# One more 512-column projection through seven half-size products, and eight small products of linear attention put in another order

## The chip, the cores and the metric

The kernel runs on one core of a Trainium2 chip (trn2). The metric is device microseconds of one execution of the whole program, the median of several runs. Inputs, weights and output lie in the chip's memory; the core works from its on-chip memory (SBUF), with matmul results in PSUM. Five engines run side by side, each through its own queue in order: TensorE (PE, with its weight loads shown apart as PEld), VectorE (DVE), ScalarE (ACT), GpSimd (POOL) and SyncE (SP), which only issues transfers.

## The reference

One layer on 512 tokens of width 1024, all in float32. What matters here:

```
h = rmsnorm(x)
hq, hk, hv, hr, ha, hatt, hgate = split(h @ w_in)
# A: gated linear attention, chunks of 64 tokens, 4 heads (dk 128, dv 256)
attn = where(causal, q_dec @ k_in.T, 0);  o = attn @ v + q_dec @ state
# B: dilated attention, 3 head groups with dilation 1, 4, 16, 4 heads each
logits = q @ k.T * hd**-0.5 + bias; softmax; @ v; groups merged by their denominators
x = x + (sigmoid(gA) * (oA @ w_o_gla) + sigmoid(gB) * (oB @ w_o_attn)) @ w_out
x = x + relu(rmsnorm(x) @ w_mlp1)**2 @ w_mlp2
x = x + sigmoid(rmsnorm(x) @ w_pg) * (p @ w_pp);  out = rmsnorm(x)
```

"The second group's keys" (k1) are the 512 columns of `h @ w_in` that give the keys of the group with dilation 4.

## The kernel before, in words

Every large product is made in three passes: both operands are split into a high and a low part (`hi` on ACT by a copy to float32r, `lo` on DVE by a subtraction), and hi·hi, hi·lo and lo·hi are added up in PSUM.

A projection of 512 columns is done in one of two ways. `fm` makes one 128-column tile at a time: 8 pieces of the contraction x 3 passes = 24 matmuls of 128x128 weights with 512 moving columns, so 96 for four tiles. `strassen` makes the whole projection as a 2x2 block product by seven half-size products (`STAGES`: A11·B11, S1·T1, A22·T4, S2·T2, A12·B21, S4·B22, S3·T3): each stage is 24 matmuls of 128x128 weights with 256 moving columns, 168 in all. S1 to S4 are sums of weight blocks, T1 to T4 sums of blocks of the normalised input. The T's are made once, by the generator `xsums`, and used by all such projections. Results of the stages stand in four PSUM banks; ACT copies one out after stages 1 to 4 (`begin`), DVE adds the second half (`finish`, in `heads` by `add`).

Weights come as 512 KB units through a ring of `NRAW` = 6 buffers, in the order of `OPERANDS`. `fetch(i+2)`, called as operand i's matmuls begin, issues `lo` of operand i+2, `hi` of i+3, weight sums of i+4 (`sums`) and the load of i+5 (`prepare`). For a projection with seven products, `EARLY` puts the load of block A21 and, on POOL, an adding transfer of A22 into the same buffer (S1) five operands ahead. `sums` makes S2 and S4 on DVE in place, and S3 by an adding transfer on POOL.

Smaller work runs as generators in the list `side`: after each piece of 8 matmuls `run` calls `step`, which takes one step of one generator (two take turns) and pops one item from `later`. `drain()` issues all that is left. So each engine's order is fixed by this program order.

The order around the change: q0 (group 0's queries, begun while the input is read), k0, then `scores0` (group 0's scores: 8 pieces of PE work, each followed by a softmax on DVE and ACT) and `xsums` go on `side`; q1 and k1 run by `fm` under them (`qk_cls`, lines 989 and 990); a drain; q2 and k2 by `heads`/`strassen`; then `scores12`, which reads q1, k1, q2, k2. At the start, POOL's power operation (line 375) gives the scale of the first normalisation; its broadcast goes through the two matmuls of lines 410 and 411.

In `gla` (once for each of the four heads) the chunk scores take eight float32 matmuls of 64 moving columns into `pa`: four with 128 weight columns (line 889) and four with 64 (line 891), in turn. A float32 matmul shows as two records in the trace.

Of the kernel before, what the change touches and what calls it, by code (L numbers as in the profile page):

```python
# [14 lines left out]
OP = mybir.AluOpType  # L15
# [19 lines left out]
def att_col(g, which):  # L35
    return ATT + (g * 3 + which) * 512
# [5 lines left out]
def weight_units():  # L42

    u = []

    def fm(name, src, col, n, row=0):
        for j in range(n):
            u.append((f"{name}.{j}", "fm", src, row, col + j * P))

    def tm(name, src, col):  # L50
        for i in range(4):
            u.append((f"{name}.{i}", "tm", src, i * 2 * P, col))

    fm("q0", "w_in", att_col(0, 0), 4)
    u = u[NS:]
    def quad(name, src, col, kind="quad"):
        for m, k in ((0, 0), (1, 0), (1, 1), (0, 1)):
            u.append((f"{name}.A{m + 1}{k + 1}", kind, src, k, col + m * (P if kind == "quad" else 256)))

    fm("k0", "w_in", att_col(0, 1), 4)  # L60
    fm("q1", "w_in", att_col(1, 0), 4)
    fm("k1", "w_in", att_col(1, 1), 4)
    quad("q2", "w_in", att_col(2, 0))
    quad("k2", "w_in", att_col(2, 1))
    quad("v1", "w_in", att_col(1, 2), "quadt")
    quad("v2", "w_in", att_col(2, 2), "quadt")
    quad("v0", "w_in", att_col(0, 2), "quadt")
    quad("gq", "w_in", GQ)
    quad("gk", "w_in", GK)
    quad("gv0", "w_in", GV, "quadt")  # L70
    for j in range(4):
        u.append((f"oa.{j}", "half", "w_o_attn", 0, j * 2 * P))
    quad("r0", "w_in", GR)
    quad("gv1", "w_in", GV + 512, "quadt")
    quad("r1", "w_in", GR + 512)
    for i in range(2):
        quad(f"gb{i}", "w_in", GATE + D + i * 512)
    for i in range(2):
        quad(f"ga{i}", "w_in", GATE + i * 512)
    fm("og", "w_o_gla", 0, 8)  # L80
    fm("wo", "w_out", 0, 8)
    for q in range(8):
        quad(f"m1q{q}", "w_mlp1", q * 512)
    for sub in range(2):
        for kk in range(16):
            u.append((f"m2s{sub}.{kk}", "tm", "w_mlp2", kk * 2 * P, sub * 512))
    for j in range(2):
        u.append((f"pp{j}.0", "tm", "w_pp", 0, j * 512))
    for j in range(2):
        tm(f"pg{j}", "w_pg", j * 512)  # L90
    return u
# [50 lines left out]
def block_kernel(ctx, tc, xT, ws, pT, wts, wha, wa2, vec, lnf, rel, onehot, ident_d, mask_d, out):  # L142
    nc = tc.nc
    V, S, TE, SY, GP = nc.vector, nc.scalar, nc.tensor, nc.sync, nc.gpsimd
# [11 lines left out]
    def u32(name="u"):  # L156
        return ar.tile([P, T], F32, tag="u", name=name)

    def u32r(name="ur"):
        return ar.tile([P, T], F32R, tag="u", name=name)  # L160
# [8 lines left out]
    side, later = [], []  # L169
# [13 lines left out]
    def drain():  # L183
        while side or later:
            step()
# [20 lines left out]
    def sums(i):  # L206
        q, _, what = OPERANDS[i].rpartition(".")
        if what == "S2":
            w = raw[f"{q}.S2"] = raw[f"{q}.S1"]
            V.tensor_tensor(w, w, raw[f"{q}.A11"], op=OP.add)  # L210

            w = raw[f"{q}.S3"] = raw[f"{q}.A11"]
            GP.dma_start(w, wts[UNIT[f"{q}.A21"]], accum_op=OP.add)  # L213
        elif what == "S4":
            w = raw[f"{q}.S4"] = raw[f"{q}.S2"]
            V.tensor_tensor(w, w, raw[f"{q}.A12"], op=OP.add)  # L216
# [73 lines left out]
    def halves(t):  # L290
        return slice(t * HT, (t + 1) * HT)
# [52 lines left out]
    def split_hi(x, col=None):  # L344
        hi = u32r()
        if col is None:
            S.activation(hi, x, AF.Copy)  # L347
        else:
            S.activation(hi, x, AF.Copy, scale=col)
        return hi  # L350

    def split_lo(x, hi, col=None):
        lo = u32r()
        if col is None:
            V.tensor_tensor(lo, x, hi.bitcast(F32), op=OP.subtract)  # L355
        else:
            V.scalar_tensor_tensor(out=lo, in0=x, scalar=col, in1=hi.bitcast(F32), op0=OP.mult, op1=OP.subtract)
        return hi, lo
# [64 lines left out]
    for k in range(KC):  # L423
        t = u32()
        SY.dma_start(t[:, 0:NS * P + 1], ws[k])
        wr.append(t)
        t = u32()
# [23 lines left out]
    for k in range(KC):  # L451
        x, ln = xr[k], wr[k][:, NS * P:NS * P + 1]
        hi, lo = u32r(), u32r()
# [27 lines left out]
    xn, xs, tx = [], [None] * KC, {}  # L481
# [12 lines left out]
    def minus(o, a, b):  # L494

        V.scalar_tensor_tensor(out=o, in0=a, scalar=-1.0, in1=b, op0=OP.mult, op1=OP.subtract)

    def xsums():
        for g in range(2):
            t1, t2, t3, t4 = (u32() for _ in range(4))  # L500
            for p in range(2):
                x0, x1 = (xn[4 * g + 2 * p + k][0] for k in range(2))
                o = halves(p)
                V.tensor_tensor(t1[:, o], x0[:, halves(0)], x0[:, halves(1)], op=OP.subtract)
                minus(t2[:, o], t1[:, o], x1[:, halves(1)])
                yield
                V.tensor_tensor(t3[:, o], x1[:, halves(1)], x0[:, halves(1)], op=OP.subtract)
                minus(t4[:, o], t2[:, o], x1[:, halves(0)])
                yield
            names, ts, hi = ("T1", "T2", "T3", "T4"), (t1, t2, t3, t4), [split_hi(t1)]  # L510
            for i in range(4):
                if i < 3:
                    hi.append(split_hi(ts[i + 1]))
                tx[names[i], g] = split_lo(ts[i], hi[i])
                yield

    def xs_op(name, pr):
        if name in ("B11", "B21", "B22"):
# [74 lines left out]
    def qk_cls(name, scale):  # L593

        res = []
        for j in range(4):
            o, ps = u32(), fm(f"{name}.{j}", xs)
            S.activation(c3(o), cm(ps), AF.Copy, scale=scale)
            res.append(o)
        return res  # L600

    def heads(name, scale, cls=False):

        res = [u32() for _ in range(4)]

        def finish(m, t, s, ps):
            for n in range(2):
                o, a, b = res[2 * n + m], s[:, halves(n)], ps[:, halves(n)]
                if cls:
                    o, a, b = c3(o)[:, :, t * 64:(t + 1) * 64], cm(a), cm(b)  # L610
                else:
                    o = o[:, halves(t)]
                add(m, o, a, b, scale)

        strassen(name, xs_op, finish, scale=scale)
        return res
# [85 lines left out]
    def scores0():  # L702
        for h in range(4):
            for bp in range(2):
                ps = smt()
                for a in range(2):
                    b = 2 * bp + a
                    lo = 0 if b else P
                    TE.matmul(ps[:, a * 256 + lo:a * 256 + 256], lhsT=q0[h][:, b * P:(b + 1) * P],  # L709
                              rhs=k0[h][:, (b - 1) * P + lo:(b + 1) * P], start=True, stop=True)  # L710
                yield
                pr = u32()
                softmax(ps, P if bp == 0 else 0, bias0[h], st0[:, 0, :], st0[:, 1, :], h * 4 + bp * 2, pr)
                p0.append(pr)
# [130 lines left out]
    def gla(h):  # L845
        b, q, k = gb_[h], gq[h], gk[h]
# [5 lines left out]
                        op=OP.subtract)  # L852
        V.tensor_tensor(ea8[:, 1::2, :], b8[:, 1::2, 63:64].to_broadcast([P, 4, 64]), b8[:, 1::2, :],
                        op=OP.subtract)
# [33 lines left out]
        for p in range(4):  # L888
            TE.matmul(pa[:, p * P + 64:(p + 1) * P], lhsT=kx[:, p * P:(p + 1) * P],  # L889
                      rhs=q[:, p * P + 64:(p + 1) * P], start=True, stop=True)  # L890
            TE.matmul(pa[0:64, p * P:p * P + 64], lhsT=k[:, p * P:p * P + 64],  # L891
                      rhs=q[:, p * P:p * P + 64], start=True, stop=True)
        qh = split_hi(qp)
# [90 lines left out]
    q0 = [qk0_evac(p, HD_SCALE) for p in q0ps + [q0t]]  # L984
    k0 = [qk0_evac(fm(f"k0.{j}", xsr), 1.0) for j in range(4)]
    drain()
    side.append(scores0())
    side.append(xsums())
    q1 = qk_cls("q1", HD_SCALE)
    k1 = qk_cls("k1", 1.0)  # L990
    drain()
    q2 = heads("q2", HD_SCALE, True)
    k2 = heads("k2", 1.0, True)
    drain()
# [91 lines left out]
    for j in range(KC):  # L1086
        t = u32()
# [83 lines left out]
    def quad(q):  # L1171


        def finish(m, t, s, ps):
            add(m, s, s, ps)

            def positive():
                V.tensor_scalar(s, s, 0.0, None, op0=OP.max)  # L1178

            def act():  # L1180
                for n in range(2):
                    j = 4 * q + 2 * n + m
                    if hid[j] is None:
                        hid[j] = u32()
                    S.activation(hid[j][:, halves(t)], s[:, halves(n)], AF.Square)  # L1185

            later.extend([positive, act])

        def extra(i):
            if i in (3, 4):  # L1190
                later.append(lambda: hid_split(i - 3))

        strassen(f"m1q{q}", x1_op, finish, extra=extra if q == 7 else None)
# [14 lines left out]
    for sub in range(2):  # L1208
        pss = [mmt() if sub == 0 else smt() for _ in range(4)]
        for kk in range(16):  # L1210
# [11 lines left out]
            if sub == 1 and kk == 8:  # L1222
                for k in range(2):
                    t = u32()
                    GP.dma_start(t, pT[k * P:(k + 1) * P, :])
                    pt.append(split(t))
                for g in range(2):
                    t = u32()
                    GP.dma_start(t, lnf[:, g * 512:(g + 1) * 512].to_broadcast([P, 512]))
                    lnb.append(t)  # L1230
        for o in range(4):
            j = 4 * sub + o
            t = u32()
# [189 lines left out]
```

## Time and profile before

| | |
|---|---|
| median of 3 runs | 979.17 us (978.92 to 979.62) |
| profiled execution, its own time | 979.68 us |
| its span in the trace | 977.9 us |
| mean granted TensorE clock | 0.998 |
| PE busy / PEld busy | 968.3 us (99%) / 885.3 us (91%) |
| DVE / ACT / POOL busy | 685.9 us (70%) / 522.6 us (53%) / 94.6 us (10%) |
| memory traffic | 133.63 MB, mean 137 GB/s |

The span runs from the first to the last instruction in the trace; the execution's own time has 1.78 us more around it. A line "L250 PE MATMUL mmt<-ur,hi" is a matmul issued by line 250 into tile mmt from tiles ur and hi. In the timeline the columns are start, duration, engine and line, and "x2" means two records merged. A matmul's recorded duration overlaps its neighbours', so the pace of PE is read from starts.

### The profile page before, as it was taken

What the parts mean: (1) busy time and instruction counts of PE and PEld (TensorE: products, weight loads), DVE (VectorE), ACT (ScalarE), POOL (GpSimd) and SP (SyncE); (2) the same over time, 40 slices, a digit from 0 to 9 for tenths busy, and PEclk for the clock granted to TensorE, in tenths of its full rate; (3) what the DMA queues carried; (4) which work ended last, traced back from release to release, by engine and by line L of the source; (5) the groups of instructions that cost most, each with busy time, mean ns of one, the idle gap of its engine ahead of it and who ended that gap; (6) DMA issues with size and microseconds to landing.
All of it is one profiled execution on the core that took longest, in us unless ns stands there. A gap on an engine that the chain in (4) does not pass through costs nothing.

```text
span 977.9 us, 15875 instructions
## 1 busy us (share of the span) xinstructions
PE 968.3 (99%) x6372; PEld 885.3 (91%) x6372; DVE 685.9 (70%) x975; ACT 522.6 (53%) x875; POOL 94.6 (10%) x135
## 2 busy tenths in 40 slices
PE   9999999999999999999999999999999999999997
PEld 7788999999998999999988889999998888888886
DVE  7777579676788769978955698777676546653654
ACT  7345546445657566665733446566565435442633
POOL 0230010420001021003010000001000000000000
PEclk9999999999999999999999999999999999999999
DMA  8463555864346545546535427565644232523102
GB/s 298 129 218 104 130 132 129 236 197 130 108 114 187 152 111 150 127 133 191 155 99 202 127 51 210 131 155 162 174 132 133 87 108 65 172 87 107 44 1 86
DMA packets 40026, 133.63 MB, mean 137 GB/s; under 512 B 5203, under 2 KB 6815, under 8 KB 39952
## 3 DMA queue, kind: packets, MB, share of 16 engines
q1 hardware_dynamic: 27936, 93.29, 28.7%
q0 software_dynamic: 10720, 36.96, 18.4%
q10 hardware_dynamic: 1296, 2.36, 0.6%
q8 instruction: 50, 0.82, 0.3%
q14 instruction: 24, 0.20, 0.1%
HBM read 126.26 MB, written 8.17 MB: 137 GB/s over the span
## 4 chain that ended last, share of the span: by engine, by line
PE 96%; DVE 2%; issue 1%; DMA 1%; ACT 0%; SPq 0%; POOLq 0%; POOL 0%; DVEq 0%
PE mmt L250 77%; PE smt L250 9%; PE smt L843 1%; PE smt L783 1%; PE smt L709 1%; PE smt L889 1%; PE mmt L468 1%; DMA u<-in_xT_dram 1%; PE mmt L469 0%; DVE lo L231 0%; PE mmt L467 0%; PE smt L891 0%; DVE ur L355 0%; PE smt L680 0%; PE smt L800 0%
## 5 line engine op out<-in xcount | busy, mean ns | idle before, releaser
L250 PE MATMUL mmt<-ur,hi 128*128 128x256 f32 (+1 forms) x2784 | 605.3, 313 | 0.0
L250 PEld LDWEIGHTS mmt<-ur,hi 128*128 128x128 f32 x2784 | 455.6, 188 | 32.2 <-issue 1.9
L250 PE MATMUL mmt<-ur,lo 128*128 128x256 f32 (+1 forms) x1392 | 436.3, 313 | 0.8 <-DVE lo L231 0.8
L231 DVE TENSOR_TENSOR lo<-w,hi 128x1024 fp32r<-128x1024 f32 x236 | 286.8, 1221 | 113.8 <-PE mmt L250 67.4
L236 ACT ACTIVATE hi<-w 128x1024 fp32r<-128x1024 f32 x236 | 247.1, 1054 | 125.0 <-issue 73.1
L250 PEld LDWEIGHTS mmt<-ur,lo 128*128 128x128 f32 x1392 | 262.3, 188 | 16.7 <-DVE lo L231 1.2
L250 PE MATMUL mmt<-hi,ur 128*128 128x256 f32 (+3 forms) x736 | 154.8, 307 | 0.0
L347 ACT ACTIVATE ur<-u 128x512 fp32r<-128x512 f32 x136 | 79.9, 621 | 84.3 <-DVE u L1078 30.9
L250 PEld LDWEIGHTS mmt<-hi,ur 128*128 128x128 f32 x736 | 118.7, 189 | 5.4
L250 PE MATMUL mmt<-lo,ur 128*128 128x256 f32 (+3 forms) x368 | 112.9, 307 | 0.0
L355 DVE TENSOR_TENSOR ur<-u,ur 128x512 fp32r<-128x512 f32 x135 | 89.0, 687 | 20.9 <-ACT ur L347 20.3
L322 ACT ACTIVATE u<-mmt 128x512 f32<-128x512 f32 x92 | 54.6, 593 | 57.1 <-PE mmt L250 57.1
L250 PE MATMUL smt<-ur,hi 128*128 128x512 f32 x272 | 83.9, 390 | 0.0
L340 DVE TENSOR_TENSOR u<-u,mmt 128x512 f32<-128x512 f32 (+1 forms) x92 | 57.8, 655 | 33.0 <-PE mmt L250 32.9
L250 PEld LDWEIGHTS mmt<-lo,ur 128*128 128x128 f32 x368 | 69.5, 189 | 2.6
L250 PEld LDWEIGHTS smt<-ur,hi 128*128 128x128 f32 x272 | 51.1, 188 | 10.6
L250 PE MATMUL smt<-ur,lo 128*128 128x512 f32 x136 | 53.1, 390 | 0.0
L213 POOL DMA_DIRECT2D w<-in_wts_dram x23 | 20.4, 886 | 286.2 <-DVE w L210 154.8
L202 POOL DMA_DIRECT2D w<-in_wts_dram x23 | 20.4, 886 | 216.8 <-DMA w<-in_wts_dram 48.5
L1185 ACT ACTIVATE u<-u 128x256 f32<-128x256 f32 x64 | 23.0, 410 | 30.5 <-DVE u L1178 30.5
L250 PEld LDWEIGHTS smt<-ur,lo 128*128 128x128 f32 x136 | 25.6, 188 | 5.2
L216 DVE TENSOR_TENSOR w<-w 128x1024 f32<-128x1024 f32 x23 | 28.2, 1225 | 0.8
(206 smaller groups left out, 714.4 us busy)
## 6 DMA issues: line engine op xcount, KB each, us to landing
w<-in_wts_dram SPq DMA_DIRECT2D x167, 512.0 KB, 4.0
w<-in_wts_dram POOLq DMA_DIRECT2D x46, 512.0 KB, 5.5
u<-in_xT_dram SPq DMA_DIRECT2D x8, 256.0 KB, 4.9
v_dram<-u POOLq DMA_DIRECT2D x8, 256.0 KB, 6.7
u<-v_dram POOLq DMA_DIRECT2D x8, 256.0 KB, 7.4
y_dram<-u ACTq DMA_DIRECT2D x8, 256.0 KB, 2.8
u<-y_dram POOLq DMA_DIRECT2D x8, 256.0 KB, 5.9
u<-in_xT_dram POOLq DMA_DIRECT2D x8, 256.0 KB, 7.4
```

The source lines that it names most:

```text
L202: GP.dma_start(w, wts[UNIT[f"{q}.A22"]], accum_op=OP.add)
L213: GP.dma_start(w, wts[UNIT[f"{q}.A21"]], accum_op=OP.add)
L216: V.tensor_tensor(w, w, raw[f"{q}.A12"], op=OP.add)
L231: V.tensor_tensor(lo, w, hi.bitcast(F32), op=OP.subtract)
L236: S.activation(hi, w, AF.Copy)
L250: TE.matmul(o, lhsT=l, rhs=r, start=a, stop=b, skip_group_check=shared)
L322: S.activation(sums[c], bank[b], AF.Copy, scale=-scale if c[0] else scale)
L340: V.tensor_tensor(out, s, ps, op=OP.subtract if m else OP.add)
L347: S.activation(hi, x, AF.Copy)
L355: V.tensor_tensor(lo, x, hi.bitcast(F32), op=OP.subtract)
L468: TE.matmul(q0ps[i], lhsT=hi[:, c], rhs=xl, start=False, stop=False)
L1185: S.activation(hid[j][:, halves(t)], s[:, halves(n)], AF.Square)
```

## The change

Keys k1 go from `fm` to `heads`/`strassen` like q2 and k2, so their weights are laid out and fetched as blocks. The T sums, which k1 now needs too, are made during q1: `xsums` is written anew to make each sum and its split for both halves before the next. `scores0` joins `side` after q1 instead of before it, and the drain between k1 and q2 is gone. In `gla` the four products with 128 weight columns come first and the four with 64 after them.

```diff
-    fm("k1", "w_in", att_col(1, 1), 4)
+    quad("k1", "w_in", att_col(1, 1))
...
     def xsums():
...
+        t1, t2, t3, t4 = ([u32(), u32()] for _ in range(4))
+        def x(g, p, k, t):
+            return xn[4 * g + 2 * p + k][0][:, halves(t)]
+        def sums(f):
+            for g in range(2):
+                for p in range(2):
+                    f(g, p, halves(p))
                 yield
+        def splits(name, ts):
+            his = [split_hi(ts[0]), split_hi(ts[1])]
+            yield
+            for g in range(2):
+                tx[name, g] = split_lo(ts[g], his[g])
+            yield
+        yield from sums(lambda g, p, o: V.tensor_tensor(t1[g][:, o], x(g, p, 0, 0), x(g, p, 0, 1), op=OP.subtract))
+        yield from splits("T1", t1)
+        yield from sums(lambda g, p, o: minus(t2[g][:, o], t1[g][:, o], x(g, p, 1, 1)))
+        yield from sums(lambda g, p, o: minus(t4[g][:, o], t2[g][:, o], x(g, p, 1, 0)))
+        yield from splits("T4", t4)
+        yield from splits("T2", t2)
+        yield from sums(lambda g, p, o: V.tensor_tensor(t3[g][:, o], x(g, p, 1, 1), x(g, p, 0, 1), op=OP.subtract))
+        yield from splits("T3", t3)
...
         for p in range(4):
             TE.matmul(pa[:, p * P + 64:(p + 1) * P], lhsT=kx[:, p * P:(p + 1) * P],
                       rhs=q[:, p * P + 64:(p + 1) * P], start=True, stop=True)
+        for p in range(4):
             TE.matmul(pa[0:64, p * P:p * P + 64], lhsT=k[:, p * P:p * P + 64],
                       rhs=q[:, p * P:p * P + 64], start=True, stop=True)
...
     drain()
-    side.append(scores0())
     side.append(xsums())
     q1 = qk_cls("q1", HD_SCALE)
-    k1 = qk_cls("k1", 1.0)
-    drain()
+    side.append(scores0())
+    k1 = heads("k1", 1.0, True)
     q2 = heads("q2", HD_SCALE, True)
     k2 = heads("k2", 1.0, True)
     drain()
```

More of the change, by code (lines that the diff above doesn't have):

```diff
@@ L498, in xsums @@
     def xsums():
[L499 to L505, printed above, removed]
-                yield
[L507 to L515, printed above, removed]
+        t1, t2, t3, t4 = ([u32(), u32()] for _ in range(4))
[5 more added lines that the diff above has]
+                    f(g, p, halves(p))
+                yield
+        def splits(name, ts):
[12 more added lines that the diff above has]
+        yield from splits("T3", t3)
     def xs_op(name, pr):
```

## The prediction

> **What bounds the kernel.** I read the page's busy shares and its chain that ended last, then the list of waits, then PE's timeline at the places that the change touches.
>
> ```profile
> PE 968.3 (99%) x6372; PEld 885.3 (91%) x6372; DVE 685.9 (70%) x975; ACT 522.6 (53%) x875; POOL 94.6 (10%) x135
> PE 96%; DVE 2%; issue 1%; DMA 1%; ACT 0%; SPq 0%; POOLq 0%; POOL 0%; DVEq 0%
> ...
> PE mmt L250 <- DVE lo L231: 0.8, 2, 0.5
> ```
>
> PE is 96% of the chain and has waited for DVE's `lo` for 0.8 us in all. So whatever shortens PE's own sequence shortens the run, if the other engines keep up; a late operand costs only what is left of its lead. A busy PE is no proof of peak pace, so I take paces from starts.
>
> **k1 itself.** Old pace inside k1, and new pace from q2 and k2, which already run as seven products:
>
> ```profile
> 92.46 0.62 PE L250 MATMUL mmt<-ur,hi 128*128 128x512 f32 x2
> ...
> 105.38 0.62 PE L250 MATMUL mmt<-ur,hi 128*128 128x512 f32 x2
> ...
> 106.07 0.41 PE L250 MATMUL mmt<-ur,hi 128*128 128x256 f32 x2
> ...
> 146.40 0.40 PE L250 MATMUL mmt<-hi,ur 128*128 128x256 f32 x2
> ```
>
> 92.46 to 105.38 is 19 groups of three: 12.92/57 = 0.2267 us a matmul. 106.07 is q2's first matmul, 146.40 the first of v1: 40.33/336 = 0.1200 us. So k1 goes from 96 x 0.2267 = 21.76 to 168 x 0.1200 = 20.16 us, -1.60 us. Halving the columns does not quite halve the pace (0.1133 would), so of the eighth of the work that is saved (2.72 us) 1.12 is lost again. q2 to k2 passes without a gap in that 40.33, so I give the new transition k1 to q2 nothing.
>
> By the gap formula in the Trainium skill (TensorE: Matmul & The Clock Gate, Back-to-back issue gap: N/2.4 + 2.5 ns when warm) the two paces would be 0.2158 and 0.1092 us and, as an estimate from that page, k1 would save 2.4 us, which makes the total 974.6 where the rows make it 975.4. The trace is slower at both sizes, by unequal amounts, so I keep the rows.
>
> **scores0 moved from q1 and k1 into k1 alone.** Chain of waits, start and duration, old place and a comparable case between 256-column matmuls (`scores12`):
>
> ```profile
> 58.15 0.65 PE smt L709 x4
> 58.80 3.65 PE mmt L250 x16
> ...
> 66.99 0.65 PE smt L709 x4
> ...
> 148.41 1.92 PE mmt L250 x16
> ...
> 153.08 1.92 PE mmt L250 x16
> ```
>
> 58.15 to 66.99 is 8.84 us with 32 matmuls (7.25), so a pair of pieces costs 1.59. The pieces stream 4 x 384 and 4 x 512 columns; at 2.4 columns per ns (0.2267 us for 512 is 2.26, just under) that is 1.49, so entering and leaving cost 0.05 a piece. `scores12`: 4.67 us less 24 x 0.12 = 1.79 for 4096 columns (1.71), 0.04 a piece. Equal: the move costs PE 0, bounds ±0.05 x 8 = ±0.4.
>
> For DVE the move crowds k1. Rows of VectorE groups between 58.2 and 106.05 us (count, busy, mean ns), and of k2's `finish`:
>
> ```profile
> L231 DVE TENSOR_TENSOR lo<-w,hi 128x1024 fp32r<-128x1024 f32 x9 | 11.0, 1218 | 1.6 <-ACT hi L236 1.6
> L355 DVE TENSOR_TENSOR ur<-u,ur 128x512 fp32r<-128x512 f32 x11 | 7.3, 686 | 6.5 <-ACT ur L347 6.4
> L660 DVE TENSOR_REDUCE st<-u 128x2 f32<-128x512 f32 x4 | 2.7, 686 | 0.1
> L659 DVE TENSOR_TENSOR u<-smt,u 128x512 f32<-128x512 f32 x4 | 2.7, 686 | 1.4 <-PE smt L709 1.4
> L657 DVE TENSOR_REDUCE st<-u 128x1 f32<-128x256 f32 x4 | 1.7, 420 | 0.1
> L507 DVE TENSOR_TENSOR u<-u 128x256 f32<-128x256 f32 x4 | 1.7, 418 | 0.0
> L656 DVE TENSOR_TENSOR u<-smt,u 128x256 f32<-128x256 f32 x4 | 1.7, 414 | 0.0
> L656 DVE TENSOR_TENSOR u<-smt,u 128x128 f32<-128x128 f32 x4 | 1.2, 288 | 3.6 <-DMA u<-cb_dram 2.8 <-PE smt L709 0.8
> L657 DVE TENSOR_REDUCE st<-u 128x1 f32<-128x128 f32 x4 | 1.1, 286 | 0.1
> ...
> L340 DVE TENSOR_TENSOR u<-u,mmt x8: 604/624/633, 140.8 to 148.2; 128x256 f32<-128x256 f32 x8
> ```
>
> In k1's window DVE has 7 `lo` (8.5), two weight sums of the same size (2.4), all of `scores0`'s softmax (2.7+2.7+1.7+1.7+1.2+1.1 = 11.1), the last sum and split of `xsums` (T3: 1.7 + 2 x 0.69 = 3.1) and four `finish` halves (2.5): 27.6 us, against PE's 20.16 + 4 x 1.59 = 26.5. DVE falls behind by 1.1 us over the whole window; counted stage by stage, which puts six of the eight softmaxes in stages 2 to 4, the backlog peaks near 2 us. `lo` is issued two stages ahead (each 2.9 to 5 us here, so over 6 us), so PE does not see it: 0. ACT, the less busy of the two on the page, has the shorter list there too. In q2 DVE catches up. `scores0`'s results are read only after v2. The first piece of `scores0` no longer waits for the bias (the 2.8 us of DMA in the row above), because it comes 22 us later.
>
> **xsums inside q1.** q1 has 12 steps; T1, T4 and T2 take exactly 12, T3 four more, taken in turn with `scores0`: done by k1's step 7 of 21, and first read in stage 7 (step 19). On DVE q1 gets 12 half sums (5.0), six splits (4.1), four `lo` (4.9) and a weight sum (1.2): 15 of 21.8 us. Cost 0. One cover shrinks: q1's first tile needs the last split of the normalised input.
>
> ```profile
> 58.90 1.47 DVE L355 TENSOR_TENSOR ur<-u,ur 128x512 fp32r<-128x512 f32 x2
> ...
> 56.17 0.62 PE L250 MATMUL mmt<-ur,hi 128*128 128x512 f32 x2
> ```
>
> q1 starts at 56.17 and uses that split in its 23rd matmul, 22 x 0.2267 later, at 61.16 without the 0.65 us of `scores0` between; it is ready at 60.37. Margin 0.8 us, so 0; if DVE is x later there, PE loses x - 0.8.
>
> **The weights of k1.** Six transfers of 512 KB instead of four, 1 MB more over the 48 us of q1 and k1, 22 GB/s; PE waits for no transfer of weights anywhere in the list of waits: 0 on the chain. But two move far ahead: five operands before k1 is k0.3, so A21's load and POOL's adding transfer of A22 are now issued before q0.3's matmuls, ahead of POOL's power operation.
>
> ```profile
> 14.33 0.33 SPq L193 DMA_DIRECT2D w<-in_wts_dram  x1
> ...
> DMA to landing us min/median/max: 3.3/5.4/8.7
> ...
> L202 POOL DMA_DIRECT2D w<-in_wts_dram x1 | 0.9, 896 | 7.2 <-DVE st L660 7.2
> ...
> 25.74 0.16 DVE L374 TENSOR_SCALAR rv<-smt 128x4 f32<-128x4 f32 x1 [0.87 <-PE smt L387]
> 25.98 1.02 POOL L375 TENSOR_TENSOR rtok<-rv,mh 128x4 f32<-128x4 f32 x1 [24.41 <-DVE rv L374]
> 28.42 0.69 DVE L355 TENSOR_TENSOR ur<-u,ur 128x512 fp32r<-128x512 f32 x1 [0.70 <-ACT ur L347]
> 29.34 0.39 PE L410 MATMUL smt<-ur,ones_r 128*128 128x512 f32 x1
> ```
>
> A21 takes the fifth issue, at 14.33; at the longest landing of that stretch it is there at 23.0, POOL issues for 0.9 us and is free at 23.9, 2 us before it is wanted. PE has 0.2 us more (29.11 to 29.34). Cost 0, and x beyond 2.2 us costs PE x. The ring loses one slot, so q1.0's load waits for a buffer until about 22.6 instead of going out at 14.7; its first reader is ACT at 37.5. 0.
>
> **The chunk scores.** PE and PEld at the first of four heads (starts 312.15, 315.57, 395.78, 400.19, alike):
>
> ```profile
> 312.15 0.33 PE L889 MATMUL smt<-u 128*128 128x64 f32 x2
> 312.41 0.33 PE L891 MATMUL smt<-u 128*64 128x64 f32 x2
> 312.67 0.43 PE L889 MATMUL smt<-u 128*128 128x64 f32 x2
> 313.03 0.33 PE L891 MATMUL smt<-u 128*64 128x64 f32 x2
> ...
> 314.54 0.50 PE L250 MATMUL mmt<-ur,lo 128*128 128x512 f32 x1
> ...
> 312.41 0.13 PEld L891 LDWEIGHTS smt<-u 128*64 128x64 f32 x1
> 312.41 0.19 PEld L891 LDWEIGHTS smt<-u 128*64 128x64 f32 x2
> 312.67 0.30 PEld L889 LDWEIGHTS smt<-u 128*128 128x128 f32 x2
> 312.52 0.22 PE L891 MATMUL smt<-u 128*64 128x64 f32 x1
> ```
>
> A wide pair holds PE 0.36 us, a narrow one 0.26. Within a wide pair the second load (0.19 alone) begins 0.11 after the first; so of 0.36, 0.11 is the step inside and 0.25 the step from wide to narrow. Within a narrow pair the second matmul starts 0.11 after the first (312.52) and its load 0.06 after, so 0.15 of the 0.26 is the step from narrow to wide. At a change of shape the next load does not run ahead. Reordered: the 16 records have 7 steps wide to wide, one to narrow, 7 narrow to narrow, and the old last step: 0.77 + 0.25 + 0.77 + 0.15 = 1.94, where four pairs of each now make 2.48. Saved 0.54 a head; 0.89 if narrow steps shrink to 0.06. Below, nothing: no row shows three loads of one shape here in a row. I take 0.55, what the nearest starts say: 4 x 0.55 = -2.2 us (0 to -3.6).
>
> **Sum:** -1.6 - 2.2 = -3.8 us: 979.68 becomes 975.9 in the profiled execution's terms. That execution is 0.5 us above the median, 979.17, so the forecast is 975.4. The measurement can tell about 0.2%, 2 us.
>
> **Rivals.** (1) The reorder gives nothing, only k1 does: 977.6. For it: loads may wait for the matmul in flight whatever the shape, with the pair's 0.11 just the two halves of one float32 product. Against it: loads of 188 ns run at 120 ns pace in q2. The Trainium skill speaks for it (same page, Part 3, The mechanism: weight loads overlap with running matmuls only when the row group differs); by that rule the wide loads would not overlap either. The overlap in q2 disagrees with it. 12%. (2) k1's gain is lost to DVE: if the backlog passes 6 us instead of 2, each further microsecond is PE's; losing all 1.6 leaves 977.0. Against: DVE's surplus is 1.1 us. 8%. (3) Slower: POOL's adding transfer, queued ahead of the power operation, waits for A21. If A21 landed at 31 instead of 23, the matmul of line 410 would be 6 us late and the whole 981.2; it decides from a landing 5.8 us past 25.2 on. Against: the longest landing would have to double. 6%.
>
> **How the numbers follow.** Both parts work: 74%, 975.4 (973.8 to 976.3 by 0 to ±0.4 for the pieces of `scores0` and 0.89 a head). Faster by over 0.2%: 74% and most of (2), so 0.78; within: (1) and the rest, 0.16; slower 0.06. The range 973.8 to 977.7 leaves out (3) and the tails.
>
> **What would show it.** In the trace after: k1's 168 matmuls at 0.120 us without a wait for `lo`; POOL's power operation still near 26 us; q1's first tile without a gap; chunk scores of a head in 1.5 to 1.95 us instead of 2.39. The prediction is wrong if wide-to-wide steps show 0.2 us, or if PE waits in k1.

## The result, and the profile after

The changed kernel takes 973.80 us (median, 973.57 to 974.23); the kernel before ran at 979.16 beside it. The ratio is 0.9946, interval 0.9933 to 0.9959: 5.4 us faster. The profiled execution took 974.23 us, span 972.4, against 979.68 and 977.9. One execution among all that follow, the profiled one of k1_only, ran its matmuls at half pace (span 1933.9 us); it is left out, and that kernel's trace is taken from a second run of it.

The page's busy shares and chain have the same form as before, and the row for `lo` in the list of PE's waits is the same:

```profile
PE 963.5 (99%) x6444; PEld 885.8 (91%) x6444; DVE 694.8 (71%) x988; ACT 524.9 (54%) x878; POOL 96.6 (10%) x137
PE 96%; DVE 2%; issue 1%; DMA 1%; ACT 0%; SPq 0%; POOLq 0%; POOL 0%; DVEq 0%
```

```profile
PE mmt L250 <- DVE lo L231: 0.8, 2, 0.5
```

The list has no wait that was not there before, so the time came from PE's own sequence. PE's timeline at q1's first matmul, k1's first and v1's first and at a head's chunk scores (now lines 899 and 902), and below it the chain at a pair of pieces of `scores0` (now line 719):

```profile
56.06 0.61 PE L250 MATMUL mmt<-ur,hi 128*128 128x512 f32 x2
...
77.83 0.41 PE L250 MATMUL mmt<-ur,hi 128*128 128x256 f32 x2
...
144.30 0.40 PE L250 MATMUL mmt<-hi,ur 128*128 128x256 f32 x2
...
309.98 1.00 PE L899 MATMUL smt<-u 128*128 128x64 f32 x8
310.91 0.68 PE L902 MATMUL smt<-u 128*64 128x64 f32 x8
311.52 0.50 PE L250 MATMUL mmt<-ur,lo 128*128 128x512 f32 x1
311.85 0.63 PE L250 MATMUL mmt<-ur,hi 128*128 128x512 f32 x2
```

```profile
79.91 0.66 PE smt L719 x4
...
82.46 0.86 PE smt L719 x4
83.33 1.92 PE mmt L250 x16
```

From q1's first to v1's first matmul: 88.24 us. Before, q1's first was the row at 56.17 and v1's the one at 146.40: 90.23. So this stretch gave 1.99. q1 itself now takes 21.77 for its 96 matmuls, the old pace of 0.2268 each. Of the 66.47 us behind it, 504 matmuls at 0.12 are 60.48, which leaves 5.99 for the eight pieces of `scores0`, where four pairs made 6.34 before (a pair, 79.91 to 83.33, is now 3.42 less 16 x 0.12 = 1.92, so 1.50 instead of 1.59). k1's pace gave 1.60 and `scores0` 0.35; the 0.04 that is left of the 1.99 is within the rounding of the paces.

A head's chunk scores went from 2.39 us to 1.54, counted to the large matmul right behind them. How soon the large matmuls get going again hangs on the last small product too (0.34 us behind a narrow one here, 0.315 behind a wide one in all_wide), so from here on the measure runs to the start of the next pair hi·hi, hi·lo: 312.15 to 314.88 before (2.73), 309.98 to 311.85 now (1.87). That is 0.86 a head, 3.44 for four. 1.99 + 3.44, and 0.1 by which the start happened to be earlier, make up the 5.5 us between the spans.

### The profile page after: what moved, and what is told of

It is laid out like the page before. It is cut to its first block, busy times and chain, and to the rows that moved or that the text cites. A ratio compares the mean times of both kernels' runs of the same rounds, so it can differ in the third digit from the quotient of the medians.

```text
span 972.4 us, 16047 instructions
## 1 busy us (share of the span) xinstructions
PE 963.5 (99%) x6444; PEld 885.8 (91%) x6444; DVE 694.8 (71%) x988; ACT 524.9 (54%) x878; POOL 96.6 (10%) x137
## 4 chain that ended last, share of the span: by engine, by line
PE 96%; DVE 2%; issue 1%; DMA 1%; ACT 0%; SPq 0%; POOLq 0%; POOL 0%; DVEq 0%
PE mmt L250 78%; PE smt L250 10%; PE smt L853 1%; PE smt L793 1%; PE smt L719 1%; PE mmt L468 1%; DMA u<-in_xT_dram 1%; PE mmt L469 0%; DVE lo L231 0%; PE mmt L467 0%; DVE ur L355 0%; PE smt L810 0%; PE smt L690 0%; PE smt L809 0%; PE smt L799 0%
## 5 line engine op out<-in xcount | busy, mean ns | idle before, releaser
L250 PEld LDWEIGHTS mmt<-ur,hi 128*128 128x128 f32 x2832 | 460.4, 188 | 30.0 <-issue 1.9
L231 DVE TENSOR_TENSOR lo<-w,hi 128x1024 fp32r<-128x1024 f32 x239 | 290.1, 1220 | 108.5 <-PE mmt L250 63.6
L236 ACT ACTIVATE hi<-w 128x1024 fp32r<-128x1024 f32 x239 | 250.0, 1054 | 130.1 <-issue 73.1
L250 PEld LDWEIGHTS mmt<-ur,lo 128*128 128x128 f32 x1416 | 266.7, 188 | 15.6 <-DVE lo L231 1.2
L322 ACT ACTIVATE u<-mmt 128x512 f32<-128x512 f32 x96 | 57.0, 593 | 54.2 <-PE mmt L250 54.1
L340 DVE TENSOR_TENSOR u<-u,mmt 128x512 f32<-128x512 f32 (+1 forms) x100 | 62.2, 650 | 32.2 <-PE mmt L250 32.1
L213 POOL DMA_DIRECT2D w<-in_wts_dram x24 | 21.4, 893 | 278.3 <-DVE w L210 166.3
L202 POOL DMA_DIRECT2D w<-in_wts_dram x24 | 21.6, 901 | 237.8 <-DVE lo L231 50.2
```

Source lines behind the costliest of these rows:

```text
L202: GP.dma_start(w, wts[UNIT[f"{q}.A22"]], accum_op=OP.add)
L231: V.tensor_tensor(lo, w, hi.bitcast(F32), op=OP.subtract)
L236: S.activation(hi, w, AF.Copy)
L250: TE.matmul(o, lhsT=l, rhs=r, start=a, stop=b, skip_group_check=shared)
L322: S.activation(sums[c], bank[b], AF.Copy, scale=-scale if c[0] else scale)
L340: V.tensor_tensor(out, s, ps, op=OP.subtract if m else OP.add)
```

## The experiments

**k1 alone** and **the order alone**, the two parts of the change:

```diff
 k1_only: the changed kernel, with the old order in gla
-        for p in range(4):
             TE.matmul(pa[0:64, p * P:p * P + 64], ...
 order_only: the kernel before, with the new order in gla
+        for p in range(4):
             TE.matmul(pa[0:64, p * P:p * P + 64], ...
```

> The changed kernel with the chunk scores in the old, alternating order: only k1's part of the change. Read from the two traces: k1 saves 1.60 us of PE pace and the pieces of scores0 cost 0.35 us less between 256-column matmuls, so 1.95 to 2.1 us below the kernel before (977.1), a head's eight products still 2.39 us. Rival, by the recorded prediction's own sum: 1.6 us (977.6). Second rival, that the larger share of the 5.4 us comes from k1 (a hidden stall that went): 975 or less.

> The kernel before with only the chunk scores reordered. Theory: each head's eight products take 1.54 us instead of 2.39, four times 0.85 = 3.4 us, all of it on the chain: 975.8. Rival, by the recorded prediction's sum: 2.2 us (977.0), the rest of the fall belonging to k1.

k1 alone: 977.13 us, ratio 0.9981 (0.9972 to 0.9990). The order alone: 976.45, ratio 0.9974 (0.9963 to 0.9985), its profiled execution 975.68. The first hits its theory; the second lies between its theory (975.8) and its rival (977.0), and the trace decides. The second run of k1_only:

> The kernel of k1_only once more, for its trace alone: from q1's first matmul to v1's first 88.24 us as in the changed kernel (90.23 before), a head's eight products as before. Rival: more than 2.1 us gained outside the chunk scores.

977.14 us. PE's timeline of that run, then of order_only:

```profile
55.61 0.62 PE L250 MATMUL mmt<-ur,hi 128*128 128x512 f32 x2
...
143.84 0.39 PE L250 MATMUL mmt<-hi,ur 128*128 128x256 f32 x2
...
309.52 0.33 PE L899 MATMUL smt<-u 128*128 128x64 f32 x2
...
311.91 0.50 PE L250 MATMUL mmt<-ur,lo 128*128 128x512 f32 x1
```

```profile
311.57 1.00 PE L889 MATMUL smt<-u 128*128 128x64 f32 x8
312.50 0.68 PE L892 MATMUL smt<-u 128*64 128x64 f32 x8
...
313.44 0.63 PE L250 MATMUL mmt<-ur,hi 128*128 128x512 f32 x2
```

q1 to v1 is 88.23 us with a head's scores still at 2.39; and the reorder alone takes a head to 1.87 as in the changed kernel. The two parts add up: by the traces 2.0 + 3.4 = 5.4 us, all of the fall; by the medians 2.0 + 2.7 = 4.7, with intervals wide enough for either.

**What in the order costs.** Two kernels that change only the four pairs, both on the kernel before. In all_wide the second product loads twice as many weights as it needs; the extra rows of its result are never read.

```diff
 all_wide
-            TE.matmul(pa[0:64, p * P:p * P + 64], lhsT=k[:, p * P:p * P + 64],
+            TE.matmul(pa[:, p * P:p * P + 64], lhsT=k[:, p * P:(p + 1) * P],
 two_runs
-        for p in range(4):
-            (wide p)
-            (narrow p)
+        for two in ((0, 1), (2, 3)):
+            for p in two: (wide p)
+            for p in two: (narrow p)
```

> The kernel before, alternating as before, but the second product of each pair loads 128 weight columns instead of 64 (the extra half of its output rows is written and never read), so no product differs in shape. Theory, that the change of weight shape is what costs (0.25 us from wide to narrow, 0.15 back, 0.11 from wide to wide): 16 records at 0.11 = 1.8 us a head although more weights are loaded, 0.6 less than before, 2.4 us in all: 976.8. Rival, that turning between two pairs of operands or two places in the result is what costs: 2.4 us a head or more, 979.2 or above.

> The kernel before with the chunk scores as two wide, two narrow, two wide, two narrow: four changes of shape on the way instead of eight or two. Theory, a fixed price for each pair of changes (0.85/3 = 0.28 us): 1.54 + 0.28 = 1.82 us a head, 2.3 us in all: 976.9. Rival, that the gain needs a long row of equal loads (the loads run ahead only after several of a kind): 2.1 us a head or more, 978 or above.

all_wide took 976.33 us, ratio 0.9972 (0.9961 to 0.9983); two_runs 976.86, ratio 0.9978 (0.9969 to 0.9986). PE's timeline at the first head of all_wide with two rows of its weight loads, and then two_runs:

```profile
311.50 0.33 PE L889 MATMUL smt<-u 128*128 128x64 f32 x2
311.66 0.39 PE L891 MATMUL smt<-u 128*128 128x64 f32 x2
...
313.51 0.63 PE L250 MATMUL mmt<-ur,hi 128*128 128x512 f32 x2
...
311.61 0.30 PEld L891 LDWEIGHTS smt<-u 128*128 128x128 f32 x2
311.83 0.30 PEld L889 LDWEIGHTS smt<-u 128*128 128x128 f32 x2
```

```profile
313.05 0.55 PE L890 MATMUL smt<-u 128*128 128x64 f32 x4
313.53 0.45 PE L893 MATMUL smt<-u 128*64 128x64 f32 x4
...
315.21 0.63 PE L250 MATMUL mmt<-ur,hi 128*128 128x512 f32 x2
```

To the next pair of large matmuls: all_wide 2.01 us, two_runs 2.16, against 2.73 and 1.87. all_wide turns between the same operands and the same columns of the result as the kernel before and loads more weights, yet is 0.72 faster a head (2.9 in all; the medians say 2.8, its theory said 2.4). Only the width of the weights changed, and with it the rows of the result, so the change of that shape is the cause. two_runs has one round trip more than the new order and costs 0.29 more; the old order has three more and costs 0.86, 0.29 each. The price goes by the number of changes, and no long row of equal loads is needed. The load rows show the change itself: in all_wide the load at 311.61 begins about 0.05 us ahead of its matmul at 311.66, while in the changed kernel the first narrow load begins only with its matmul, at 310.91:

```profile
310.91 0.54 PEld L902 LDWEIGHTS smt<-u 128*64 128x64 f32 x8
```

The Trainium skill (TensorEngine Tiling (Array Packing), Tiling Modes) says that changing the tiling mode drains TensorE and lists 128x64 as a mode of its own. That a product with 64 weight columns runs in that mode is shown by no run here; if it does, these traces agree.

**Two heads' scores together**, on the changed kernel: the even head leaves its operands and the odd head issues both (in outline).

```diff
+        waiting[h] = (kx, k, q)
+        if h % 2:
+            for i in (h - 1, h): (four wide products of head i)
+            for i in (h - 1, h): (four narrow products of head i)
...
+        while h not in pas:
+            yield
```

> The changed kernel with the chunk scores of two heads issued together: eight wide products (sixteen records), then eight narrow ones, so two changes of shape for two heads instead of four. By the price that the runs so far give (0.28 us for a pair of changes) one pair less for each two heads, 0.57 us in all: 973.2 against 973.8, less than the time can tell; in the trace two heads' scores take 0.28 us less. Rival: the head that waits for its neighbour is one step later, its sums come later, and PE waits for them: 974 or more.

973.76 us, ratio 0.9939 (0.9925 to 0.9952). The chain, first the changed kernel's two heads, then this one's:

```profile
308.29 1.85 PE mmt L250 x8
310.14 0.84 PE smt L899 x8
310.98 0.61 PE smt L902 x8
311.59 1.12 PE mmt L250 x4
...
314.15 4.76 PE mmt L250 x20
```

```profile
308.67 2.77 PE mmt L250 x12
311.44 1.73 PE smt L907 x16
313.17 1.07 PE smt L912 x16
314.24 4.78 PE mmt L250 x20
```

5.86 us become 5.57 for two heads: the price again, 0.29. About 0.6 us in all stands in the trace; the time alone can't tell it from the changed kernel. It is the fastest of these kernels by ratio, with an interval that overlaps. The doubling also gives the steady steps: eight more wide records cost 0.89 (0.11 each), eight more narrow ones 0.46 (0.058).

**scores0 beside 256-column matmuls**, the kernel before with one line moved:

```diff
-    side.append(scores0())
     side.append(xsums())
...
+    side.append(scores0())
     q2 = heads("q2", HD_SCALE, True)
```

> The kernel before with one move: scores0 joins the side work after the drain behind k1, so its eight pieces of PE work stand between the 256-column matmuls of q2 instead of the 512-column ones of q1 and k1. Theory: a pair of pieces costs 1.50 us there instead of 1.59, the eight pieces 6.0 us instead of 6.34, so the stretch from q1's first matmul to v1's first is 0.35 us shorter (89.9 us instead of 90.23) and the time 978.8, no difference that the time alone can tell. Rival, that those 0.35 us in the changed kernel came from another part of k1's conversion: 6.34 us and 90.23.

978.79 us, ratio 0.9996 (0.9987 to 1.0006). Timeline at q1's and v1's first matmul, and the chain from the first piece to past the last:

```profile
55.73 0.62 PE L250 MATMUL mmt<-ur,hi 128*128 128x512 f32 x2
...
145.61 0.40 PE L250 MATMUL mmt<-hi,ur 128*128 128x256 f32 x2
```

```profile
100.38 0.65 PE smt L709 x4
...
113.13 33.59 PE mmt L250 x280
```

145.61 - 55.73 = 89.88, 0.35 less than before with k1 untouched; 12.75 us less seven pieces of eight matmuls (6.72) leave 6.03 for `scores0`. So the 0.35 belongs to the neighbours of these products and not to k1. The chain of the kernel before shows where it lay:

```profile
63.32 3.68 PE mmt L250 x16
```

The pieces themselves take 0.65 and 0.86 us in both places. But the 16 matmuls of 512 columns behind a piece take 3.65 or 3.68 us, where 16 x 0.2267 is 3.63, while 16 of 256 columns take 1.92 or 1.89, where 16 x 0.12 is 1.92. In the single records of the kernel before, the first ten or so matmuls behind a piece start up to 0.236 us apart: 0.27 us for the eight pieces, most of the 0.35. Why they do stays open.

**How much DVE may fall behind**, on the changed kernel, with 7 and with 18 scalings of a scratch tile behind k1's fifth stage (in outline):

```diff
+        if i == 4:
+            d = u32()
+            V.memset(d, 1.0)
+            for _ in range(7):    # dve8: 18
+                V.tensor_scalar(d, d, 1.0, None, op0=OP.mult)
```

> The changed kernel with about 3.3 us of idle work added on VectorE behind k1's fifth stage (a memset and seven scalings of a scratch tile that nobody reads). Theory from the changed kernel's trace: VectorE has no gap from 93 to 112 us and its low weight part for q2's third stage is ready only 1.4 us before that stage begins (1.6 before its first use), so PE loses 3.3 - 1.6 = 1.7 us: 975.5. Rival, by the recorded prediction's reckoning (a lead of over 6 us less a backlog of 2): PE loses nothing, 973.8.

> The same with eighteen scalings, about 8 us of idle work on VectorE. Theory: PE loses 8 - 1.6 = 6.4 us: 980.2. Rival, by the recorded prediction's reckoning: 8 - 4 = 4 us: 977.8. Third, that later gaps of VectorE take it up before anyone waits: 973.8.

dve3: 973.92 us, ratio 0.9947 (0.9930 to 0.9964), no loss. dve8: 979.72, ratio 1.0006 (0.9997 to 1.0016). DVE's timeline of dve3, then of dve8 the timelines of DVE and PE and, by stretches of time, the busy time of each engine and the granted clock (after the length: PE, PEld, DVE, ACT, POOL, PEclk):

```profile
98.90 3.20 DVE L1006 TENSOR_SCALAR u<-u 128x512 f32<-128x512 f32 x7
```

```profile
99.06 8.27 DVE L1006 TENSOR_SCALAR u<-u 128x512 f32<-128x512 f32 x18
107.35 1.23 DVE L231 TENSOR_TENSOR lo<-w,hi 128x1024 fp32r<-128x1024 f32 x1
...
108.63 0.39 PE L250 MATMUL mmt<-ur,lo 128*128 128x256 f32 x1 [4.01 <-DVE lo L231]
```

```profile
108.00:110.00 2.00, 1.37 (x8) 1.37 (x9) 2.00 (x4) 0.00 (x0) 0.00 (x0) 0.79 0.01 4
110.00:112.00 2.00, 2.00 (x11) 2.00 (x10) 1.97 (x3) 0.00 (x0) 0.00 (x0) 0.50 0.00 0
112.00:114.00 2.00, 2.00 (x16) 2.00 (x16) 2.00 (x4) 1.88 (x2) 0.86 (x1) 0.85 0.00 0
```

3.7 us of added work (0.48 of it the memset in front) are free. Of 8.8, PE waited for 4.0, so the lead was 4.7 us. The changed kernel's own rows agree: the low part for q2's first stage is ready at 99.39 and first used at 104.22.

```profile
98.17 1.22 DVE L231 TENSOR_TENSOR lo<-w,hi 128x1024 fp32r<-128x1024 f32 x1
...
104.22 0.28 PE L250 MATMUL mmt<-ur,lo 128*128 128x256 f32 x1
```

So the recorded reckoning (over 6 less 2) held, and my later reading of 1.6 was wrong, because I had put each low part one stage too early. By the time alone dve8 looks like that reading's 980.2, but that is chance: the wait was 4.0 and not 6.4, and the run lost 5.9 because the clock fell too (below).

**POOL's early transfer**, one operand later on the changed kernel (in outline):

```diff
-        if i in EARLY:                      # k1: i == 4
+        if i == 5: raw[name] = load(name)   # q1.0 first, then k1's early pair
```

> The changed kernel with k1's early pair (the load of A21 and POOL's adding transfer of A22) issued one operand later, behind q1.0's load, still ahead of POOL's power operation. A21's load then has to wait for a free buffer (22.5 us) and lands 4 to 8 us later. Theory: POOL waits for it, the power operation starts at 28 to 31 us instead of 25.9, the matmul of line 410 with it, and PE loses that less 0.2 us: 2 to 5 us, most likely 3.5: 977.3. Rival, that PE has other work there and the delay is hidden: 973.8.

975.29 us, ratio 0.9961 (0.9948 to 0.9974). POOL's and PE's timelines, the changed kernel first:

```profile
21.52 1.08 POOL L202 DMA_DIRECT2D w<-in_wts_dram  x1 [19.94 <-DMA w<-in_wts_dram]
25.88 1.04 POOL L375 TENSOR_TENSOR rtok<-rv,mh 128x4 f32<-128x4 f32 x1 [3.27 <-DVE rv L374]
...
29.46 0.39 PE L411 MATMUL smt<-ur,ones_r 128*128 128x512 f32 x1
```

```profile
26.60 1.08 POOL L205 DMA_DIRECT2D w<-in_wts_dram  x1 [25.02 <-DMA w<-in_wts_dram]
27.47 1.39 POOL L378 TENSOR_TENSOR rtok<-rv,mh 128x4 f32<-128x4 f32 x1
...
30.30 0.49 PE L413 MATMUL smt<-ur,ones_r 128*128 128x512 f32 x1 [1.03 <-ACT ur L350]
31.03 0.50 PE L414 MATMUL smt<-ur,ones_r 128*128 128x512 f32 x1 [0.23 <-DVE u L542]
```

The load landed at 26.6, at the early end of what was expected, so the run lost 1.5 us instead of 3.5. The path is as told: a transfer that POOL waits for, a power operation behind it 1.6 us late, and the second of PE's two matmuls (line 411, here 414) 1.6 us late: PE has next to no cover.

## Why the prediction was right, and which term was off

The direction and the mechanism held. The forecast, 975.4, was 1.6 us too high: 3.8 us were forecast and 5.4 came. The time, 973.8, lies on the lower edge of the range, and that it does not lie below it is partly luck: both terms that could go lower went nearly as far as they were allowed to (-0.35 of -0.4, and 0.86 a head of 0.89), and those two bounds together give 975.4 - 0.4 - 1.36 = 973.6, not the 973.8 that was written.

- k1 itself: -1.60 forecast from the paces 0.2267 and 0.1200; both are found again, and k1_only's second run shows the stretch 2.0 us shorter with `scores0`'s part.
- `scores0` moved: taken as 0, bounds ±0.4; it gave -0.35. The old price was taken for entering and leaving the pieces and compared with `scores12`, whose pieces cost 0.04 each; but most of it was the slower 512-column matmuls behind each piece, and beside k1 `scores0` pays almost nothing over its own columns (1.50 for a pair, where 1.49 was reckoned).
- The chunk scores: the term that was mis-sized. Of the two prices for a narrow-to-narrow step I took 0.11, from the start of the second matmul of a pair, and kept 0.06, from its load, for the edge (0.89 a head). heads_joined measures 0.058, and a head gained 0.86. The term was -2.2 and is -3.4.
- Costs taken as 0: `xsums` in q1, the shrunken cover at q1's first tile, the weights, the ring. No wait of PE appears for any.
- DVE in k1's window (k1's matmuls run from 77.83 to 103.98 in the changed kernel; columns as above):

```profile
77.80:104.30 26.50, 26.50 (x204) 25.84 (x203) 24.06 (x41) 19.92 (x48) 1.73 (x2) 1.00 0.39 100
```

  Busy 24.1 of 26.5 us where 27.6 had been counted: about 1.0 of T3's sums and 0.7 of the last `lo` fall outside, and the records overlap each other by 1.9. The lead held, with 4.7 us left.
- POOL at the start: free at 22.6 us where 23.9 had been bounded, and the power operation did not move. PE's 0.2 us of cover was read against line 410, but the split that is ready at 29.11 is the operand of line 411, 0.23 later. As a rival the path was real (pool_late) but far off.
- The rival that the reorder gives nothing fell: order_only is 2.7 us faster, and wide loads run 0.11 us apart in all_wide (two from 311.61, the next two from 311.83), though each lasts 0.19, and begin before their matmuls. The rule of the Trainium skill that stood for it (TensorE: Matmul & The Clock Gate, Part 3, The mechanism) does not hold for these loads.

## What to carry to other kernels

When small products with full and with half weight columns alternate, put equal shapes together, even across independent pieces of work; padding the narrow ones to full width also beats alternating. To count what such an order will gain, read the step between equal shapes from the starts of the loads, not from those of the first two matmuls behind a change: in the kernel before the loads of a pair start 0.108 (wide) and 0.055 us (narrow) apart, their matmuls 0.160 and 0.107, and in long rows both go at 0.112 and 0.058. Before another engine is given more work in one stage, count its lead in microseconds and test it by adding idle work.

## What the runs showed of the hardware that I had not expected

Between float32 products of 64 moving columns, a change from 128 to 64 weight columns and back costs PE 0.29 us over the steady steps (0.11 wide, 0.058 narrow). And a stall can cost more than its length: behind 4.0 us without a matmul in dve8 the granted clock stood at 0.50 for about 3.4 us (the three stretches lack 0.21, 0.50 and 0.15 of 2 us each, 1.72 us in all, half of 3.4). The profiled run's span is 5.6 us longer than the changed kernel's, 1.6 more than the wait; the other runs of dve8 had mean clocks of 0.994 to 0.996 as well, where the changed kernel has 0.997 or 0.998. The Trainium skill (TensorE: Matmul & The Clock Gate, Part 1) describes such a gate with windows of 3.4 us; this trace agrees.
